# Hybrid encoder trunk, 2 layers on one core: three sets of transposes move from TensorE to Vector

## The chip, the cores and the metric

One core of a Trainium2 chip runs the whole program. The metric is the device time of one execution in microseconds, median of the runs; the kernel before takes 2178.41 us (3 runs, 2178.34 to 2178.55). Lower is better. TensorE, Vector (DVE), Scalar (ACT), GpSimd (POOL) and the DMA queue of SyncE each work through their own instructions in program order and wait for one another by semaphores.

## The reference

`x` is 256 tokens by 2048 channels in float32. Each of the 2 layers has a token mixer and a gated feed-forward part. The mixer's input projection feeds four groups whose outputs are laid side by side and multiplied with `w_out`:

```python
h = rmsnorm(x, norm_mix_pre[l])
proj = h @ w_in[l]
a_q, a_k, a_v, b_glu, c_q, c_k, c_v, d_q, d_k, d_v = jnp.split(proj, split_at, axis=-1)
out_a = diff_attention(a_q, a_k, a_v, diff_lambda[l], diff_subln[l], l)
out_b = conformer_conv(b_glu, ...)      # a * sigmoid(g), 31-tap depthwise conv, layernorm, silu, pointwise
out_c = gqa_axial_attention(c_q, c_k, c_v, gqa_q_norm[l], gqa_k_norm[l])
out_d = neighbourhood_attention(d_q, d_k, d_v, na_rpb[l])
mixed = jnp.concatenate([out_a, out_b, out_c, out_d], axis=-1) @ w_out[l]
x = x + rmsnorm(mixed, norm_mix_post[l])
h = rmsnorm(x, norm_ffn_pre[l])
f = (jax.nn.silu(h @ ffn_gate[l]) * (h @ ffn_up[l])) @ ffn_down[l]
x = x + rmsnorm(f, norm_ffn_post[l])
```

Group A ends in a root-mean-square norm of each head's output; group D is an attention of 4 heads of 128 with a bias. The change touches the input of B's convolution, the output of A, and D's queries and keys.

## The kernel before

**Big products.** Tokens are in two tiles of 128 (`tok` 0 and 1). Every weight slab of 128x1024 is loaded as float32 and split into two single-pass parts: Scalar writes `whi`, Vector writes the rest `wlo` (`split_hi`, `split_lo`). Activations are split in the same way. A step (`products`) is one slab by one token tile: for each of two PSUM banks hi by hi, hi by lo and lo by hi, 6 products of 128x512 into `acc`. Steps come in groups of 3 to 6 slabs, first for token tile 0 and then for tile 1; 7 split slabs are held at once (`NSPLIT`), so Vector may run some slabs ahead of TensorE. The input projection makes the groups in the order B, C, A, D, V (values of A and D); the output projection takes its rows in the order C, B, A, D (`OUT_ORDER`), and a step of it needs the whole output of its group, both token tiles.

**Work beside the products.** The groups' own work is written as generators (`glu`, `conv`, `attn_a`, `attn_d`, `head_d`, `out_a`, `out_d`, ...). After every step `tick` lets each of them issue its next piece up to its next `yield`, if a running estimate of the engines' times (`spend`) says that what it waits for is done. So the order of the instructions of every engine is fixed when the program is written, by these estimates. The 124 taps of the convolution (31 for each of 4 blocks of channels) are Vector instructions that `fill` puts in wherever Vector's estimated time is less than 1.5 us ahead of TensorE's (`CONV_LEAD`). Where a step's input isn't made yet, `wait` ticks the generators until it is, and their instructions then stand on TensorE between two steps with no product in between.

**PSUM.** 4 banks hold `acc`, 2 are for scores (`sc`), 2 for transposes and small products (`tp`); `claim` and `free` count them.

**Transposes.** What has tokens on partitions and is needed with channels on partitions is transposed on TensorE into a `tp` bank (4 blocks of 128x128), and Scalar writes it to SBUF, by Scalar and Vector together where it is split into hi and lo (`split_hi_lo`). One quarter of the tokens' normalised input is turned by Vector instead, in `post` (lines 534 to 540), in 16 instructions of 32 partitions by 128 with 32x32 blocks that go from one quadrant of partitions to another.

**Lines that the change touches.** `glu` (644): Scalar's sigmoid and Vector's product give `u`, lines 657 to 664 transpose it to `uT`, which the taps read. `attn_d` (958): `heads_transposed` makes `qkD` from `rotD`, for queries and keys and two token tiles; then each head makes scores, softmax (`softmax`), transposed probabilities `ptD`. `out_a` (1013): for each token tile the products of probabilities and values go to an `sc` bank, Scalar sums squares (`junk`), GpSimd takes the root `rs`, Vector scales to `oA`, lines 1036 to 1043 transpose and split it to `mixA`. After `conv`'s norm, 4 pointwise groups of 4 products (`tp<-conv,pw`) make `mixB`.

Of the kernel before, what the change touches and what calls it, by code (L numbers as in the profile page):

```python
# [13 lines left out]
AF = mybir.ActivationFunctionType  # L14
# [5 lines left out]
P = 128  # L20
L = 2
S = 256
T = S // P
# [7 lines left out]
PAD = TAPS // 2  # L31
# [71 lines left out]
class Trunk:  # L103
# [461 lines left out]
    def turned(self, l, j):  # L565
# [10 lines left out]
        for tok in range(T):  # L576
            self.mark("h", l, j, tok)


    def layer_consts(self, l):  # L580

        nc, a = self.nc, self.a
        lc = self.slot([2048], F32, "lc")
        v = self.v = {}
        self.l = l
        at = 0

        def part(n, shape):
            nonlocal at
            w = int(np.prod(shape))  # L590
            t = lc[:, at:at + w]
            at += w
            if len(shape) > 1:
                names = "abc"[:len(shape)]
                t = t.rearrange(f"p ({' '.join(names)}) -> p {' '.join(names)}", **dict(zip(names, shape)))
            v[n] = t
            return t

        for n in ("gqa_q_norm", "gqa_k_norm", "diff_subln"):
            part(n, (HD,))  # L600
        nc.sync.dma_start(lc[:, 0:at], a["heads"][l].partition_broadcast(P))
        first = at
        part("dw", (4, TAPS))
        for n in ("conv_dw_b", "conv_ln_g", "conv_ln_b", "conv_pw_b"):
            part(n, (4,))
        nc.sync.dma_start(lc[:, first:at], a["conv"][l])
        yield
        yield
        nc.vector.tensor_scalar(part("subln", (HD,)), v["diff_subln"], 1.0 - self.lam_init(l), None,
                                op0=ALU.mult)  # L610
        for n in ("q", "k"):
            g = v[f"gqa_{n}_norm"]
            cg, sg = part(f"cos_{n}", (T, HD)), part(f"sin_{n}", (T, HD))
            nc.vector.tensor_tensor(cg, self.rope["cos_c"], g.unsqueeze(1).to_broadcast([P, T, HD]),
                                    op=ALU.mult)
            gv = g.rearrange("p (b h w) -> p b h w", b=2, h=2)
            s4 = self.rope["sin_c"].rearrange("p t (b h w) -> p t b h w", b=2, h=2)
            o4 = sg.rearrange("p t (b h w) -> p t b h w", b=2, h=2)
            for h in range(2):
                for t in range(T):  # L620
                    nc.vector.tensor_tensor(o4[:, t, :, h], s4[:, t, :, h], gv[:, :, 1 - h], op=ALU.mult)
# [22 lines left out]
    def glu(self, phase, pair, tok):  # L644
        nc = self.nc
        if tok == 0:
            self.u = self.slot([T, 512], F32, "u")
            self.uT = self.slot([4, S + 2 * PAD], F32, "uT")
            nc.gpsimd.memset(self.uT[:, :, 0:PAD], 0.0)
            nc.gpsimd.memset(self.uT[:, :, PAD + S:], 0.0)  # L650
        av, gv = (self.acc[phase, pair, tok, b] for b in range(2))
        r = self.rstd[:, tok:tok + 1]
        u = self.u[:, tok]
        nc.scalar.activation(u, gv, AF.Sigmoid, scale=r)
        nc.vector.scalar_tensor_tensor(u, av, r, u, op0=ALU.mult, op1=ALU.mult)
        yield
        yield from self.claim("tp")
        b = self.bank("tp", (4, P))
        for c in range(4):
            nc.tensor.transpose(b[:, c], u[:, c * P:(c + 1) * P], self.ident)  # L660
        yield
        nc.scalar.activation(self.uT[:, :, PAD + tok * P:PAD + (tok + 1) * P], b, AF.Copy)
        yield
        self.free("tp")
        self.mark("u", phase)
        if tok == T - 1:
            yield from self.until(T, "u", phase)
            yield
            yield from self.conv()
# [288 lines left out]
    def attn_d(self):  # L958
        qk = self.slot([2, 4, S], F32, "qkD")
        for i in range(2):  # L960
            yield from self.heads_transposed(qk[:, i], lambda t: self.rotD[:, t, i], 4)
        self.ptD = self.slot([4, T, S], F32, "ptD")
        work = self.slot([2, 2, T, S], F32, "workD")
        for h in range(4):
            yield from self.until(h - 1, "done_d", self.l)
            self.spawn(self.head_d(h, qk, work[:, h % 2]))
            yield
# [45 lines left out]
    def out_a(self):  # L1013
        nc, v = self.nc, self.v
        yield from self.until(4, "done_a", self.l)
        self.mixT[0] = self.slot([2, 4, S], F32R, "mixA")
        for t in range(T):
            yield from self.claim("sc")
            b = self.bank("sc", (4, HD))
            for h in range(4):  # L1020
                for c in range(T):
                    nc.tensor.matmul(b[:, h], self.ptA[:, h, c, t * P:(t + 1) * P],
                                     self.vAD[:, c, 0, h * HD:(h + 1) * HD], start=c == 0, stop=c == T - 1)
            yield
            ss, rs = self.small(4, "ss"), self.small(4, "rs")
            for h in range(4):
                self.square_sum(b[:, h], ss[:, h:h + 1], (HD,))
            self.rsqrt(rs, ss, 4, 1.0 / HD)
            o = self.tmp([4, HD], "oA")
            for h in range(4):  # L1030
                nc.vector.scalar_tensor_tensor(o[:, h], b[:, h], rs[:, h:h + 1], v["subln"],
                                               op0=ALU.mult, op1=ALU.mult)
            yield
            self.free("sc")
            yield
            yield from self.claim("tp")
            b = self.bank("tp", (4, P))
            for h in range(4):
                nc.tensor.transpose(b[:, h], o[:, h], self.ident)
            yield  # L1040
            self.split_hi_lo([self.mixT[0][:, i, :, t * P:(t + 1) * P] for i in range(2)], b)
            yield
            self.free("tp")
        self.mark("mix", self.l, 0)


# [134 lines left out]
```

## Time and profile before

| | |
|---|---|
| median of 3 runs | 2178.41 us |
| profiled execution, its own time | 2178.1 us |
| its span, first to last instruction | 2175.9 us |
| TensorE busy | 2154.6 us, 99% of the span |
| Vector busy | 1300.2 us, 60% |
| Scalar busy | 1092.4 us, 50% |
| granted TensorE clock, mean | 0.999 |

The profile is of one execution. Busy times of TensorE come from modelled ends of pipelined products. The helper that records every operation gives all of them line 89, so operations are told apart by what they write and read: `out<-in` by the program's names. A transpose on TensorE is a MATMUL with `ident`; a transpose on Vector is a STREAM_TRANSPOSE. An idle time is put down to the engine whose signal came last. A float32 product of 128x256 is recorded in two parts, so a pointwise group of 4 products has x8.

### The profile page before, as it was taken

Reading aid. Unit: us, or ns where it says so; the run is one execution under the profiler, and the core shown is the slowest. Engines: PE = TensorE matmul, PEld = TensorE weight load, DVE = VectorE, ACT = ScalarE, POOL = GpSimd, SP = SyncE. Lnnn points to the kernel's source line nnn. Section 1 sums busy time; section 2 is a strip of 40 time slices with the busy share of each in tenths; the row PEclk is TensorE's granted clock in tenths of the full one; section 3 lists DMA queues with packets and bytes.
Section 4 is the critical chain, followed back from the end, with each engine's and each line's share of the span. In section 5 each row is a group of like instructions: output and inputs, shape, how many; then the busy total and the mean of one; then the engine's idle time right before and its main releaser. Section 6 shows DMA issues by size and latency. Waiting matters only on the chain.

```text
span 2175.9 us, 25246 instructions
## 1 busy us (share of the span) xinstructions
PE 2154.6 (99%) x9696; PEld 1778.7 (82%) x9696; DVE 1300.2 (60%) x1616; ACT 1092.4 (50%) x1398; POOL 29.9 (1%) x38
## 2 busy tenths in 40 slices
PE   8999999999999999999999999999999999999998
PEld 7888888888888888888878888888888888888886
DVE  5898556755546554444488974566555555454444
ACT  6656755544445444343455577555444444443432
POOL 0000000000000000000000000000000000000000
PEclk9999999999999999999999999999999999999999
DMA  7556446776776666655565563557667666665553
GB/s 277 194 176 185 170 148 223 232 219 210 225 217 220 209 226 216 220 193 193 208 225 187 193 192 136 199 188 251 213 222 223 211 215 222 222 213 213 193 219 130
DMA packets 200281, 447.52 MB, mean 206 GB/s; under 512 B 20704, under 2 KB 43744, under 8 KB 197856
## 3 DMA queue, kind: packets, MB, share of 16 engines
q1 hardware_dynamic: 200016, 445.87, 60.9%
q8 instruction: 76, 1.25, 0.2%
q14 instruction: 45, 0.37, 0.1%
q10 hardware_dynamic: 144, 0.03, 0.0%
HBM read 425.93 MB, written 19.92 MB: 205 GB/s over the span
## 4 chain that ended last, share of the span: by engine, by line
PE 95%; ACT 2%; DVE 1%; issue 1%; DMA 1%; DVEq 0%; POOLq 0%; ACTq 0%; SPq 0%
PE acc L89 91%; PE tp L89 3%; PE sc L89 1%; ACT whi L89 1%; DVE wlo L89 1%; ACT workA L89 0%; DMA lc<-in_heads_dram 0%; ACT L89 0%; DVE mx L89 0%; ACT xT L89 0%; DVE xt L89 0%; DMA x<-in_x_dram 0%; ACT conv L89 0%; ACT junk L89 0%; DVE xT L89 0%
## 5 line engine op out<-in xcount | busy, mean ns | idle before, releaser
L89 PE MATMUL acc<-whi,xT 128*128 128x512 f32 x4096 | 1292.7, 393 | 5.4 <-ACT xT L89 2.4
L89 PEld LDWEIGHTS acc<-whi,xT 128*128 128x128 f32 x4096 | 770.0, 188 | 169.5 <-ACT xT L89 3.5
L89 PE MATMUL acc<-wlo,xT 128*128 128x512 f32 x2048 | 799.4, 390 | 2.6 <-DVE wlo L89 2.6
L89 ACT ACTIVATE whi<-raw,gains 128x1024 fp32r<-128x1024 f32 x512 | 580.5, 1150 | 365.3 <-PE acc L89 334.3
L89 DVE SCALAR_TENSOR_TENSOR wlo<-raw,gains,whi 128x1024 fp32r<-128x1024 f32 x512 | 641.7, 1278 | 188.9 <-ACT whi L89 180.9
L89 PEld LDWEIGHTS acc<-wlo,xT 128*128 128x128 f32 x2048 | 385.3, 188 | 81.9 <-DVE wlo L89 4.4
L89 DVE TENSOR_TENSOR wlo<-raw,whi 128x1024 fp32r<-128x1024 f32 x240 | 292.6, 1223 | 260.5 <-ACT whi L89 243.8
L89 PE MATMUL acc<-whi,hT 128*128 128x512 f32 x1408 | 434.1, 389 | 0.0
L89 ACT ACTIVATE whi<-raw 128x1024 fp32r<-128x1024 f32 x240 | 253.7, 1061 | 304.1 <-PE acc L89 304.0
L89 PEld LDWEIGHTS acc<-whi,hT 128*128 128x128 f32 x1408 | 264.3, 188 | 55.0
L89 PE MATMUL acc<-wlo,hT 128*128 128x512 f32 x704 | 273.9, 389 | 0.0
L89 PEld LDWEIGHTS acc<-wlo,hT 128*128 128x128 f32 x704 | 132.1, 188 | 27.3
L89 DVE TENSOR_TENSOR hT<-ht,hT 128x1024 fp32r<-128x1024 f32 x22 | 27.0, 1226 | 163.5 <-ACT hT L89 163.5
L89 DVE SCALAR_TENSOR_TENSOR h<-acc,rstd,h 128x512 f32<-128x512 f32 x44 | 33.1, 751 | 113.4 <-ACT h L89 113.4
L89 DVE SCALAR_TENSOR_TENSOR conv<-uT,lc,conv 128x256 f32<-128x256 f32 x240 | 99.4, 481 | 0.0
L89 ACT ACTIVATE hT<-ht 128x1024 fp32r<-128x1024 f32 x22 | 23.3, 1059 | 128.7 <-DMA ht<-h_blocks 128.7
L89 ACT ACTIVATE h<-acc,rstd 128x512 f32<-128x512 f32 x44 | 30.3, 689 | 80.5 <-PE acc L89 80.3
L89 ACT ACTIVATE junk<-acc 128x512 bf16<-128x512 f32 x32 | 19.0, 595 | 55.9 <-PE acc L89 53.0
L89 PE MATMUL acc<-whi,mixC 128*128 128x512 f32 x128 | 44.7, 402 | 0.0
L89 DVE TENSOR_TENSOR mg<-acc,gpost 128x512 f32<-128x512 f32 x32 | 21.3, 686 | 35.8 <-PE acc L89 19.5
L89 PE MATMUL acc<-whi,mixB 128*128 128x512 f32 x128 | 42.2, 397 | 0.0
L89 PE MATMUL acc<-whi,mixD 128*128 128x512 f32 x128 | 41.6, 391 | 0.0
(139 smaller groups left out, 987.4 us busy)
## 6 DMA issues: line engine op xcount, KB each, us to landing
raw<-in_ffn_gate_dram SPq DMA_DIRECT2D x176, 512.0 KB, 3.8
raw<-in_ffn_up_dram SPq DMA_DIRECT2D x176, 512.0 KB, 5.1
raw<-in_ffn_down_dram SPq DMA_DIRECT2D x88, 1024.0 KB, 5.0
raw<-in_w_in_dram SPq DMA_DIRECT2D x63, 1024.0 KB, 5.1
raw<-in_w_out_dram SPq DMA_DIRECT2D x32, 1024.0 KB, 5.0
raw<-in_w_in_dram SPq DMA_DIRECT2D x34, 512.0 KB, 4.7
h_blocks<-blocks SPq DMA_DIRECT2D x44, 256.0 KB, 5.5
ht<-h_blocks SPq DMA_DIRECT2D x88, 128.0 KB, 6.0
```

What stands on the lines that cost most here:

```text
L89: return f(*args, **kw)
```

## The change

A new helper `turn` transposes 4 blocks of 128x128 in SBUF with 16 Vector instructions, 4 to a piece. It takes the place of TensorE's transposes, the `tp` bank and Scalar's copy in three places: `u` to `uT`, `rotD` to `qkD` (queries and keys, each token tile), and `oA` to a new temporary `oT`, from which `mixA` is split.

```diff
+    def turn(self, dst, src):
+
+        src = src.rearrange("p (k n) -> p k n", n=P)
+        for q in range(4):
+            qs = slice(32 * q, 32 * q + 32)
+            for r in range(4):
+                rs = slice(32 * r, 32 * r + 32)
+                self.nc.vector.transpose(dst[qs, :, rs], src[rs, :, qs])
+            yield
...
@@ glu
-        yield from self.claim("tp")
-        b = self.bank("tp", (4, P))
-        for c in range(4):
-            nc.tensor.transpose(b[:, c], u[:, c * P:(c + 1) * P], self.ident)
-        yield
-        nc.scalar.activation(self.uT[:, :, PAD + tok * P:PAD + (tok + 1) * P], b, AF.Copy)
-        yield
-        self.free("tp")
+        yield from self.turn(self.uT[:, :, PAD + tok * P:PAD + (tok + 1) * P], u)
@@ attn_d
-            yield from self.heads_transposed(qk[:, i], lambda t: self.rotD[:, t, i], 4)
+            for t in range(T):
+                yield from self.turn(qk[:, i, :, t * P:(t + 1) * P], self.rotD[:, t, i])
@@ out_a
-            yield from self.claim("tp")
-            b = self.bank("tp", (4, P))
-            for h in range(4):
-                nc.tensor.transpose(b[:, h], o[:, h], self.ident)
-            yield
-            self.split_hi_lo([self.mixT[0][:, i, :, t * P:(t + 1) * P] for i in range(2)], b)
-            yield
-            self.free("tp")
+            ot = self.tmp([4, P], "oT")
+            yield from self.turn(ot, o.rearrange("p h w -> p (h w)"))
+            self.split_hi_lo([self.mixT[0][:, i, :, t * P:(t + 1) * P] for i in range(2)], ot)
+            yield
```

The pieces are issued by the same estimates, so all that follows in a layer's mixer stage can be placed anew. Three places follow.

TensorE, layer 0, at the output projection's change from group C's rows to group B's. Before, one of the pointwise groups (`conv,pw`) and the transposes of a D head's probabilities (`ident,workD`) among the products of C:

```order
L89 MATMUL sc_2293<-vAD_2214,ptA_1624 128x128 x8
L89 MATMUL acc_2284<-whi_2134,mixC_1267 128x512
L89 MATMUL acc_2284<-wlo_2153,mixC_1267 128x512
L89 MATMUL acc_2285<-whi_2134,mixC_1267 128x512
L89 MATMUL acc_2285<-wlo_2153,mixC_1267 128x512
L89 MATMUL acc_2284<-whi_2134,mixC_1267 128x512
L89 MATMUL acc_2285<-whi_2134,mixC_1267 128x512
L89 MATMUL tp_2310<-conv_582,pw_1733 128x256 x4
L89 MATMUL tp_2315<-ident,workD_2145 128x128 x4
```

Afterwards, from the last product of C to the first two of B:

```order
L89 MATMUL acc_2347<-whi_2204,mixC_1289 128x512
L89 MATMUL tp_2406<-conv_674,pw_2044 128x256 x4
L89 MATMUL tp_2439<-conv_674,pw_2044 128x256 x4
L89 MATMUL tp_2448<-ident,workD_2337 128x128 x4
L89 MATMUL tp_2458<-conv_674,pw_2044 128x256 x4
L89 MATMUL sc_2463<-vAD_2189,ptA_1621 128x128 x8
L89 MATMUL tp_2472<-ident,workD_2337 128x128 x4
L89 MATMUL sc_2499<-qkD_1824 128x256 x2
L89 MATMUL tp_2502<-conv_674,pw_2044 128x256 x4
L89 MATMUL tp_2508<-ptD_2336,vAD_2189 128x256 x2
L89 MATMUL sc_2524<-qkD_1824 128x256 x2
L89 MATMUL acc_2264<-whi_2221,mixB_2405 128x512
```

All four pointwise groups moved behind the last product of C.

Vector, layer 0, the first heads of D: from the scaled scores of head 0 (`workD`) to the reciprocal of its sums (`sm`). Before:

```order
L89 SCALAR_TENSOR_TENSOR workD_2145<-sc_2164,bias_1430 128x512
L89 SCALAR_TENSOR_TENSOR mixB_2130<-tp_2173,lc_268,mixB_2130 128x256
L89 TENSOR_REDUCE mx_2190<-workD_2145 128x2
L89 TENSOR_SCALAR mx_2190<-mx_2190 128x2
L89 SCALAR_TENSOR_TENSOR workD_2145<-sc_2179,bias_1430 128x512
L89 TENSOR_REDUCE mx_2208<-workD_2145 128x2
L89 TENSOR_SCALAR mx_2208<-mx_2208 128x2
L89 SCALAR_TENSOR_TENSOR mixB_2130<-tp_2203,lc_268,mixB_2130 128x256
L89 RECIPROCAL sm_2191<-sm_2191 128x2
```

Afterwards (the reciprocal `sm_2389` is two rows further on, behind the first `mixB`):

```order
L89 SCALAR_TENSOR_TENSOR workD_2337<-sc_2354,bias_1431 128x512
L89 TENSOR_TENSOR wlo_2373<-raw_2139,whi_2357 128x1024
L89 STREAM_TRANSPOSE oT_2383<-oA_2325 32x4x32 x4
L89 TENSOR_REDUCE mx_2388<-workD_2337 128x2
L89 TENSOR_SCALAR mx_2388<-mx_2388 128x2
L89 SCALAR_TENSOR_TENSOR workD_2337<-sc_2368,bias_1431 128x512
L89 TENSOR_TENSOR wlo_2397<-raw_2225,whi_2371 128x1024
L89 STREAM_TRANSPOSE oT_2383<-oA_2325 32x4x32 x4
L89 TENSOR_REDUCE mx_2415<-workD_2337 128x2
L89 TENSOR_SCALAR mx_2415<-mx_2415 128x2
L89 TENSOR_TENSOR wlo_2423<-raw_2225,whi_2395 128x1024
```

Three splits and 8 turns of A's first token tile stand there now.

Vector, layer 1, group A's second token tile: from `oA` to `mixA`. Before:

```order
L89 SCALAR_TENSOR_TENSOR oA_10403<-sc_10365,rs_10391,lc_8239 128x128 x4
L89 TENSOR_TENSOR mixD_10231<-tp_10425,mixD_10231 128x256
L89 TENSOR_TENSOR wlo_10453<-raw_10221,whi_10378 128x1024
L89 TENSOR_TENSOR mixD_10231<-tp_10443,mixD_10231 128x256
L89 TENSOR_TENSOR mixA_10235<-tp_10446,mixA_10235 128x4x128
```

Afterwards (after these rows come another split, a reciprocal, a maximum, 8 turns in one row, a reciprocal and `mixA_10312`):

```order
L89 SCALAR_TENSOR_TENSOR oA_10532<-sc_10499,rs_10520,lc_8323 128x128 x4
L89 TENSOR_TENSOR mixD_10515<-tp_10516,mixD_10515 128x256
L89 SCALAR_TENSOR_TENSOR workD_10333<-sc_10545,bias_9438 128x512
L89 TENSOR_TENSOR wlo_10560<-raw_10292,whi_10447 128x1024
L89 STREAM_TRANSPOSE oT_10571<-oA_10532 32x4x32 x4
L89 TENSOR_REDUCE mx_10576<-workD_10333 128x2
L89 TENSOR_SCALAR mx_10576<-mx_10576 128x2
L89 SCALAR_TENSOR_TENSOR workD_10333<-sc_10555,bias_9438 128x512
L89 TENSOR_TENSOR wlo_10585<-raw_10292,whi_10558 128x1024
L89 TENSOR_TENSOR mixD_10515<-tp_10568,mixD_10515 128x256
L89 STREAM_TRANSPOSE oT_10571<-oA_10532 32x4x32 x4
L89 TENSOR_TENSOR wlo_10603<-raw_10423,whi_10583 128x1024
```

The softmax rows of D's heads 2 and 3 moved in between, with 16 turns and three more splits.

## Rows read from the trace of the kernel before

**Rows 1.** The page's busy times by engine, whole span.

```profile
PE 2154.6 (99%) x9696; PEld 1778.7 (82%) x9696; DVE 1300.2 (60%) x1616; ACT 1092.4 (50%) x1398; POOL 29.9 (1%) x38
```

**Rows 2.** Waits of TensorE, whole span: us in total, times, longest.

```profile
PE acc L89 <- DVE wlo L89: 2.6, 4, 0.9
PE acc L89 <- ACT xT L89: 2.4, 4, 0.7
```

**Rows 3.** Busy times by stage: two stretches of each layer's mixer stage.

```profile
core 0: us, PE busy (x) PEld busy (x) DVE busy (x) ACT busy (x) POOL busy (x), PEclk, DMA share, GB/s
60.00:200.00 140.00, 140.00 (x645) 115.39 (x645) 129.59 (x234) 79.40 (x130) 3.80 (x2) 1.00 0.58 192
200.00:285.00 85.00, 84.82 (x429) 70.08 (x428) 47.10 (x78) 61.71 (x128) 2.13 (x3) 1.00 0.45 153
1160.00:1280.00 120.00, 120.00 (x555) 99.16 (x554) 114.64 (x203) 70.27 (x117) 3.79 (x2) 1.00 0.59 193
1280.00:1360.00 80.00, 79.95 (x400) 65.51 (x399) 43.04 (x77) 60.56 (x127) 3.10 (x3) 1.00 0.42 145
```

**Rows 4.** Groups by line, whole span: busy us, mean ns, idle before.

```profile
L89 DVE STREAM_TRANSPOSE xt<-x 32x128 f32<-32x128 f32 x96 | 29.0, 303 | 1.5
...
L89 PE MATMUL tp<-ident,rotD 128*128 128x128 f32 x32 | 4.8, 274 | 0.0
...
L89 ACT ACTIVATE qkD<-tp 128x512 f32<-128x512 f32 x8 | 4.8, 598 | 0.0
...
L89 PE MATMUL tp<-ident,oA 128*128 128x128 f32 x16 | 2.4, 272 | 0.0
L89 PE MATMUL tp<-ident,u 128*128 128x128 f32 x16 | 2.4, 272 | 0.0
...
L89 ACT ACTIVATE mixA<-tp 128x512 fp32r<-128x512 f32 x4 | 2.3, 582 | 0.0
```

**Rows 5.** The chain of waits, 1300 to 1400 us: start, us, what.

```profile
1334.60 1.73 PE tp L89 x8
...
1354.50 0.86 PE tp L89 x4
...
1358.99 0.44 PE tp L89 x4
...
1362.63 1.39 PE acc L89 x6
1364.03 1.78 PE sc L89 x16
```

**Rows 6.** Tile mixB, 240 to 345 us: duration ns min/median/max, first and last start.

```profile
L89 PE MATMUL acc<-whi,mixB x64: 387/389/580, 284.9 to 342.3; 128*128 128x512 f32 x64
...
L89 DVE SCALAR_TENSOR_TENSOR mixB<-tp,lc,mixB x4: 476/484/485, 252.0 to 271.6; 128x256 fp32r<-128x256 f32 x4
```

**Rows 7.** Tile mixA, the same stretch and columns.

```profile
L89 PE MATMUL acc<-whi,mixA x64: 387/389/580, 298.1 to 331.4; 128*128 128x512 f32 x64
...
L89 DVE TENSOR_TENSOR mixA<-tp,mixA x2: 692/692/693, 278.6 to 292.9; 128x512 fp32r<-128x512 f32 x2
```

**Rows 8.** Timeline of Vector, 1325 to 1395 us: start, us, instruction.

```profile
1370.40 1.13 DVE L89 SCALAR_TENSOR_TENSOR oA<-sc,rs,lc 128x128 f32<-128x128 f32 x4 [1.13 <-POOL rs L89]
...
1375.98 0.69 DVE L89 TENSOR_TENSOR mixA<-tp,mixA 128x512 fp32r<-128x512 f32 x1
```

**Rows 9.** Groups of Vector by form, whole span: busy us, mean ns, idle before.

```profile
L89 DVE TENSOR_TENSOR wlo<-raw,whi 128x1024 fp32r<-128x1024 f32 x240 | 292.6, 1223 | 260.5 <-ACT whi L89 243.8
...
L89 DVE SCALAR_TENSOR_TENSOR workD<-sc,bias 128x512 f32<-128x512 f32 x8 | 5.5, 682 | 0.6 <-PE sc L89 0.5
...
L89 DVE TENSOR_REDUCE mx<-workD 128x2 f32<-128x512 f32 x8 | 5.4, 677 | 0.0
...
L89 DVE TENSOR_TENSOR mixD<-tp,mixD 128x256 fp32r<-128x256 f32 x8 | 3.4, 425 | 11.9 <-ACT mixD L89 11.9
...
L89 DVE TENSOR_SCALAR mx<-mx 128x2 f32<-128x2 f32 x16 | 2.7, 170 | 0.6
```

## The prediction

> **What bounds the kernel now.** I read the busy shares first, then what TensorE waited for, then the stages, then single stretches. TensorE is busy 99% of the span, and its waits for other engines on the products add up to a few microseconds [rows 1, 2]: the span is TensorE's own work, so what leaves it is won one for one, and any new wait of TensorE is lost one for one. Vector is busy 60% over the span, but the share by stage is what counts [rows 3]. From 60 to 200 us of the first layer it is busy 129.59 of 140 us (92.6%), because the convolution's taps are put into every gap the planner sees; from 200 to 285 us 47.10 of 85 us. The second layer repeats it: 114.64 of 120, then 43.04 of 80 us. So each layer's mixer stage has Vector nearly full first and about half free afterwards, and the half-free part is where the attention heads, the convolution's norm and the groups' outputs hand work from engine to engine.
>
> **What the change removes.** Per layer 4 transposes for each of 2 tokens of the gated input, 4 for each of 2 tokens of group A's output, and 4 for each of 2 tokens of queries and of keys of group D: 8 groups of 4. The trace has them as 16 rows of u, 16 of oA and 32 of rotD [rows 4]. One group of 4 takes 0.44 us of TensorE in the chain [rows 5], so 16 x 0.44 = 7.1 us leave the bound engine. Scalar loses the evictions of u (4) and of D (8), about 0.6 us each [rows 4], 7 us in all; A's output is still split by Scalar and Vector as before. I cost Scalar's relief at nothing: TensorE was fully busy in those stretches.
>
> **What it adds.** Each group of 4 becomes 16 Vector instructions of 32x128. The same instruction on the same shape is in the trace: 96 of them, 303 ns [rows 4]. That is 16 x 0.303 = 4.85 us per group, 8 groups a layer: 38.8 us a layer, 77.6 us in all. None of it is TensorE's, so it costs nothing as long as what Vector delivers is not late. It is a trade of 0.44 us of TensorE and 0.6 us of Scalar against 4.85 us of Vector. The Trainium skill speaks against it: VectorE: DVE Perf Modes, "Rules for kernel authors", says to transpose 128x128 on TensorE where the result may lie in PSUM. By that page's section "The three transpose paths" a TensorE transpose takes 390 ns and 64 of them 25 us, which with the waits below would give about 2169 us; the trace's 0.44 us for four decides, and the sum goes by it.
>
> **Is Vector's work hidden?** First by capacity [rows 3]. Layer 0, 60 to 285 us: 129.6 + 47.1 + 38.8 = 215.5 of 225 us, 96%. It fits only if Vector hardly waits. The most it held in the long first stretch, where the taps (which wait for nobody) fill it, is 92.6%; at that share 215.5 us take 232.7, 7.7 more than there is. Layer 1, 1160 to 1360 us: 114.6 + 43.0 + 38.8 = 196.5 of 200 us; at the 95.5% of its first stretch 205.7, 5.7 more. That is 13.4 us by which TensorE would have to wait.
>
> Then by place, with the order of the instructions. The output projection takes the groups in the order C, B, A, D. Before, in layer 0, B's last part came at 271.6 us and was first used at 284.9, A's at 292.9 + 0.7 and was used at 298.1 [rows 6, 7]: 13 and 4.5 us to spare. Afterwards the conv's taps end later, because the turns of u stand ahead of them and the turns of D among them, and A's and D's chains have turns in them.
>
> Layer 0, B. All four pointwise products now stand behind the last product of C, with no product between them, where before they were spread between products. TensorE meets three hand-overs there. (1) D's head 0: from its scores to its probabilities' transposes. Vector's queue between holds workD twice, three splits, 8 turns, two maxima and small ones: 2x0.68 + 3x1.22 + 8x0.303 + 2x0.68 + 4x0.17 = 9.5 us [rows 4, 9], and Scalar's exponentials and scalings stand between its maxima and its reciprocals; from the scores on I take 13.8 us (an estimate: Vector's 9.5 and Scalar's turns in between; the queue alone would leave 9.5 - 8.5 = 1 us of wait). TensorE's own rows between: 3 steps of 1.39, one pair of scores 0.86, two pointwise groups of 1.73 [rows 5] = 8.5. Wait 5.3 us. (2) The third pointwise group needs a transpose bank that Vector's second mixB frees, behind 8 turns and two reciprocals, 2.7 us; TensorE has one group of 0.44 to do meanwhile: wait about 2 us. (3) The last pair of scores needs the bank that oA frees; before, oA ended 7.5 us after its product began (1364.03 to 1370.40 + 1.13) [rows 5, 8], and TensorE's rows between are 1.78 + 0.44 + 0.86 + 1.73 + 0.86 = 5.7: wait 1.8 us. Sum 9.
>
> Layer 1, A. B just fits there (its pointwise groups stand two to three steps apart), and A's second token is late. From oA to mixA Vector's queue held before one split and two mixD, 1.22 + 2x0.42 = 2.1 us; now it holds three more splits, 16 turns and the softmax rows of D's heads 2 and 3: 4x1.22 + 2x0.42 + 2x0.68 + 2x0.68 + 16x0.303 + 4x0.17 = 14.0 us [rows 4, 9]. From the product on: 7.5 + 14.0 + Scalar's 0.58 = 22.1 us. TensorE's own rows from that product to the first product of A: 1.78, 6 steps of 1.39, five pairs of 0.86 and two groups of 0.44 [rows 5] = 15.4. Wait 6.7, say 7 us. The same sum for before gives 7.5 + 2.1 + 0.44 + 0.58 = 10.6, so mixA at 1374.6; the trace has it at 1375.98 [rows 8].
>
> The two ways agree: 13.4 and 16. I take 16, since the second names the places. The wait of a queue is not confined to them: behind a turn stand splits (wlo) that TensorE needs, and a softmax maximum that Scalar needs; the seven weight buffers cover a split that is a few microseconds late, and I cost that at nothing while the backlog stays under the wait above.
>
> Ends: nothing waits, all 38.8 us a layer lie in Vector's gaps: -7.1 us. Or Vector, in the second stretch, gets done only what it did before, since its gaps are others' chains and cannot be filled: 38.8 - 10.4 free in the first stretch = 28.4 us a layer, 56.8 - 7.1 = +50 us.
>
> **Sum.** -7.1 + 9 + 7 = +8.9 us. The profiled execution took 2178.1 us (span 2175.9 and 2.2 around it), the median of the runs is 2178.41, so the two can be taken as one: 2187.3 us, 2187.
>
> **Rivals.** About 0.2%, 4.4 us, is what a measurement of this kernel can tell from no change: below 2174.0 is faster, above 2182.8 slower.
> (a) All hidden: 2178.4 - 7.1 = 2171.3. For it: Vector has 37.9 us idle in 200:285 and 37 in 1280:1360 [rows 3], a layer's turns 38.8, and part goes before. Against: 4.5 us to spare at A, and the pointwise groups that moved behind the last product of C. It holds while the waits stay under 2.7 us: chance 0.08.
> (b) The waits eat the gain: the hand-overs overlap more than I reckon (one of the two places hidden, or half of each), waits 3 to 11 us, 2174 to 2183, in the middle 2178. For it: three of my hand-overs are 2 us or so each, within the error of such sums. Chance 0.17.
> (c) Forecast, waits 11.5 to 30 us: 2183 to 2201. Chance 0.57.
> (d) Vector becomes the bound of the stage: its backlog grows through the turns of D until the splits come late too, so that TensorE stops at wlo and not only at B and A. It decides from where the backlog is more than the seven buffered splits hide. For it: 96% in the stretch, and every turn is one more instruction ahead of a split. Against: in the stretch at 92.6% TensorE waited for wlo only 2.6 us in the whole span [rows 2]. Price: from 30 us of waits up to the 56.8 above, 2201 to 2228. Chance 0.18.
> Faster 0.08, same 0.17, slower 0.57 + 0.18 = 0.75. The range from 2174 to 2211 leaves out (a) and the upper half of (d), about 0.16.
>
> **What would show it.** Right: TensorE's instructions fall by 64, its busy time by some 7 us or its idle time rises past that; a row of idle time of TensorE before a pointwise product, a workD transpose or the first mixB near 285 to 300 us, and before mixA near 1375; Vector over 90% from 200 to 285 us; 256 new turns of about 303 ns. Waits for mixB or its chain should be near 9 us in layer 0 and for mixA near 7 us in layer 1. Wrong: TensorE still 99% busy with no idle row in these stretches (then a), or its idle rows named wlo, all through 200 to 300 us (then d). If a turn from quadrant to quadrant takes clearly more than 303 ns with these operands, all of Vector's sums rise with it.

## The result, and the profile after

The changed kernel takes **2202.82 us** (median of 4 runs, 2202.64 to 2202.99) against 2178.38 us before: 24.4 us slower, ratio 1.0112 with a 95% interval of 1.0095 to 1.0130. The forecast was 2187, range 2174 to 2211: slower was right, the size was 8.9 us in place of 24.4.

The page of the changed kernel, busy times and the share of each engine in the chain that ended last; the first row answers to [rows 1]:

```profile
PE 2159.8 (98%) x9632; PEld 1776.3 (81%) x9632; DVE 1377.5 (63%) x1872; ACT 1080.4 (49%) x1382; POOL 31.4 (1%) x38
...
PE 77%; DVE 15%; ACT 3%; issue 2%; DMA 2%; POOL 0%; SPq 0%; DVEq 0%; ACTq 0%; POOLq 0%
```

TensorE has 64 instructions fewer, Vector 77.3 us more, as predicted. But TensorE's busy time rose by 5.2 us although its work shrank, and its idle time (span 2200.9 less 2159.8, 41.1 us) rose by 19.8 us from 21.3. These two are the 25.0 us by which the profiled span grew.

The new turns, groups of Vector by form (busy us, mean ns | idle before):

```profile
L89 DVE STREAM_TRANSPOSE qkD<-rotD 32x128 f32<-32x128 f32 x128 | 38.7, 302 | 1.9
...
L89 DVE STREAM_TRANSPOSE uT<-u 32x128 f32<-32x128 f32 x64 | 19.5, 304 | 1.0
L89 DVE STREAM_TRANSPOSE oT<-oA 32x128 f32<-32x128 f32 x64 | 19.3, 302 | 0.9
```

What TensorE waited for in the whole span (total, times, longest), answering to [rows 2]:

```profile
PE tp L89 <- ACT workD L89: 12.8, 4, 3.9
...
PE acc L89 <- DVE wlo L89: 3.0, 4, 0.9
PE sc L89 <- ACT workA L89: 2.2, 4, 1.2
...
PE tp L89 <- ACT ptD L89: 1.6, 1, 1.6
PE tp L89 <- DVE workA L89: 1.4, 2, 1.0
```

The waits for the splits (`wlo`) hardly moved. The new ones are the probabilities of D (`workD`, which Scalar writes last, after Vector's reciprocal) and, smaller, A's softmax. Where they lie, in TensorE's timeline (start, us, instruction, idle before it and who ended that):

```profile
239.31 0.70 PE L89 MATMUL sc<-qkA 64*128 64x256 f32 x2 [1.23 <-ACT workA L89]
...
282.94 1.12 PE L89 MATMUL tp<-ident,workD 128*128 128x128 f32 x4 [3.41 <-ACT workD L89]
285.65 3.41 PE L89 MATMUL tp<-conv,pw 128*128 128x256 f32 x8 [1.59 <-ACT ptD L89]
...
290.69 0.60 PE L89 MATMUL tp<-ident,workD 128*128 128x128 f32 x4
...
295.02 1.13 PE L89 MATMUL sc<-qkD 128*128 128x256 f32 x4 [0.28 <-DVE oA L89]
...
1373.52 1.04 PE L89 MATMUL tp<-ident,workD 128*128 128x128 f32 x4 [2.91 <-ACT workD L89]
...
1396.57 0.84 PE L89 MATMUL tp<-ident,workD 128*128 128x128 f32 x4 [3.86 <-ACT workD L89]
1400.06 1.12 PE L89 MATMUL tp<-ident,workD 128*128 128x128 f32 x4 [2.65 <-ACT workD L89]
```

Two things are to be seen. The waits are at the places of the prediction (the three hand-overs at B in layer 0, and ahead of A's first product in layer 1) and at two that it did not have: A's softmax (239.31) and D's head 0 in layer 1 (1373.52). At 285.65 the profile names Scalar's `ptD`, which ended at 285.60; Vector's second `mixB`, which the prediction named, ended at 285.63, so the trace doesn't tell the two apart. And the instruction behind a wait takes longer: a pointwise group of 8 took 1.73 in the chain before [rows 5] and takes 1.89 at 291.99 here, but 3.41 behind that wait. The windows of 1 us show why (busy of TensorE, its weight loads, Vector, Scalar, GpSimd; then the granted clock):

```profile
284.00:285.00 1.00, 0.06 (x1) 0.00 (x0) 0.96 (x4) 1.00 (x3) 0.00 (x0) 0.50 0.53 209
285.00:286.00 1.00, 0.35 (x1) 0.35 (x2) 0.53 (x2) 1.00 (x3) 0.00 (x0) 0.50 0.00 0
286.00:287.00 1.00, 1.00 (x3) 0.82 (x3) 0.69 (x1) 0.12 (x1) 0.00 (x0) 0.50 0.07 16
287.00:288.00 1.00, 1.00 (x4) 0.72 (x4) 0.00 (x0) 0.00 (x0) 0.00 (x0) 0.50 0.00 0
288.00:289.00 1.00, 1.00 (x5) 0.85 (x4) 0.00 (x0) 0.00 (x0) 0.00 (x0) 0.72 0.00 0
```

The granted clock is at 0.50, the 1.2 GHz level, while TensorE is busy again. In 25 such windows of the two mixer stages it is under 0.97; busy time times the missing share of the clock adds up to 7.7 us. Before, none was under 0.97 in these stages. TensorE's busy time grew by 12.3 us beyond its work (5.2 + 7.1); with the 7.7 taken off, an estimated 4.6 are left. Four transposes behind a wait are recorded longer than four without one at the full clock too (0.84 at 1396.57, granted clock 1.00, against 0.60 at 290.69). That all of the 4.6 us lie in such groups is not shown.

Vector by stage, answering to [rows 3]:

```profile
60.00:200.00 140.00, 139.60 (x634) 114.12 (x633) 132.76 (x248) 75.04 (x119) 3.80 (x2) 1.00 0.57 189
200.00:285.00 85.00, 77.91 (x360) 61.48 (x358) 73.98 (x167) 55.77 (x118) 3.61 (x3) 0.96 0.50 173
...
1280.00:1360.00 80.00, 78.85 (x381) 62.98 (x380) 71.26 (x154) 53.27 (x113) 3.08 (x3) 1.00 0.53 182
```

In 200:285 it is 87% busy, not over 90% as predicted: it waits itself, in its own order, for instance 1.34 us for Scalar's `mixB` at 281.73.

### The profile page after: what moved, and what is told of

Read it like the earlier page. It is cut to its first block, busy times and chain, and to the rows that moved or that the text cites. A ratio compares the mean times of both kernels' runs of the same rounds, so it can differ in the third digit from the quotient of the medians.

```text
span 2200.9 us, 25365 instructions
## 1 busy us (share of the span) xinstructions
PE 2159.8 (98%) x9632; PEld 1776.3 (81%) x9632; DVE 1377.5 (63%) x1872; ACT 1080.4 (49%) x1382; POOL 31.4 (1%) x38
## 3 DMA queue, kind: packets, MB, share of 16 engines
q8 instruction: 75, 1.23, 0.2%
## 4 chain that ended last, share of the span: by engine, by line
PE 77%; DVE 15%; ACT 3%; issue 2%; DMA 2%; POOL 0%; SPq 0%; DVEq 0%; ACTq 0%; POOLq 0%
PE acc L89 76%; DVE wlo L89 6%; DVE conv L89 4%; ACT whi L89 1%; PE tp L89 1%; DVE qkD L89 1%; DVE mx L89 1%; DMA raw<-in_w_in_dram 1%; DVE oT L89 1%; ACT workA L89 1%; DVE rope L89 0%; DVE rotC L89 0%; DVE rotA L89 0%; DMA lc<-in_heads_dram 0%; DVE uT L89 0%
## 5 line engine op out<-in xcount | busy, mean ns | idle before, releaser
L89 PE MATMUL acc<-whi,mixB 128*128 128x512 f32 x128 | 44.2, 410 | 0.0
L89 DVE TENSOR_TENSOR mg<-acc,gpost 128x512 f32<-128x512 f32 x32 | 21.3, 686 | 35.7 <-PE acc L89 19.5
L89 PE MATMUL acc<-whi,mixA 128*128 128x512 f32 x128 | 41.7, 400 | 0.0
```

What stands on the lines that cost most here:

```text
L89: return f(*args, **kw)
```

## The experiments

Ratios are to the kernel before, timed in the same set; idle is TensorE's, span less busy (21.3 us in the kernel before).

| kernel | median us | to before | ratio (95%) | idle us |
|---|---|---|---|---|
| whole change | 2202.82 | +24.4 | 1.0112 (1.0095 to 1.0130) | 41.1 |
| only_u | 2183.84 | +5.6 | 1.0024 (1.0014 to 1.0035) | 25.8 |
| only_d | 2192.10 | +13.8 | 1.0062 (1.0045 to 1.0079) | 32.8 |
| only_a | 2185.86 | +7.6 | 1.0034 (1.0021 to 1.0047) | 28.1 |
| taps11 | 2191.12 | +12.8 | 1.0060 (1.0045 to 1.0075) | 35.3 |
| turn_local | 2181.30 | +2.8 | 1.0013 (1.0003 to 1.0022) | 27.7 |
| warm | 2198.72 | +20.2 | 1.0092 (1.0077 to 1.0107) | 29.1 |
| cost303 | 2226.36 | +47.8 | 1.0218 (1.0201 to 1.0235) | 57.8 |
| only_u303 | 2194.20 | +15.7 | 1.0072 (1.0057 to 1.0087) | 32.8 |
| cost_turn | 2210.50 | +32.2 | 1.0148 (1.0133 to 1.0163) | 47.0 |
| u_cost | 2182.85 | +4.5 | 1.0021 (1.0012 to 1.0031) | 26.8 |
| d_cost | 2188.21 | +9.9 | 1.0045 (1.0030 to 1.0060) | 32.4 |
| d_merge | 2208.39 | +30.1 | 1.0136 (1.0119 to 1.0153) | 44.2 |

**One part at a time.** Each kernel is the one before with the helper `turn` and one of the three edits:

```diff
 only_u:
+        yield from self.turn(self.uT[:, :, PAD + tok * P:PAD + (tok + 1) * P], u)
 only_d:
+                yield from self.turn(qk[:, i, :, t * P:(t + 1) * P], self.rotD[:, t, i])
 only_a:
+            yield from self.turn(ot, o.rearrange("p h w -> p (h w)"))
```

> Only the convolution's gated input is turned by Vector; A's output and D's queries and keys stay on TensorE. TensorE loses 4 groups of 0.44 us, 1.8 us; Vector gains 9.7 us a layer. Theory 'capacity' (the time is lost because Vector has more to do in the mixer stage than the stage is long): layer 0 then holds 176.7 + 9.7 = 186.4 us in 225, 83%, so nothing waits: 2176.6 us. Theory 'hand-overs' (the time is lost where TensorE stands at a group's output that comes late, whatever Vector's share): the planner puts three of the four pointwise groups of layer 0 behind the last product of C, as in the whole change, so TensorE waits there some 3 to 6 us, with the slow clock behind it up to 8, and hardly in layer 1, where the pointwise groups stay two steps apart: 2179 to 2184 us.

> Only D's queries and keys are turned by Vector. TensorE loses 8 groups of 0.44 us, 3.5 us; Vector gains 19.4 us a layer, the largest part. Theory 'capacity': layer 0 holds 196.1 us in 225, 87%, layer 1 177.1 in 200, 88%; nothing waits, 2174.9 us; if any part alone fills Vector it is this one. Theory 'hand-overs': the pointwise groups stay among the products as before, so B is in time in both layers; only the last heads of D move towards D's own rows (transposes of probabilities two or so behind the last product of A), a wait of 0 to 4 us a layer: 2175 to 2183 us.

> Only group A's output is turned by Vector. TensorE loses 4 groups of 0.44 us, 1.8 us; Vector gains 9.7 us a layer. Theory 'capacity': 186.4 of 225 us, 83%, and 167.4 of 200: nothing waits, 2176.6 us. Theory 'hand-overs': 0.44 us of TensorE in A's chain become at least 4.85 us of Vector, against 4.5 us to spare in layer 0 and 4 or so in layer 1, with splits and softmax rows queued between: TensorE stands before the first product of A 2 to 6 us a layer, with the slow clock behind it up to 8: 2180 to 2192 us.

Each part alone is slower, by 5.6, 13.8 and 7.6 us, together 27.0 against 24.4 for the whole. "Capacity" fails in all three, most clearly in only_d, which it put at 2174.9. "Hand-overs" holds for u (2179 to 2184; its waits at B are 1.14, 1.42, 1.01 and 0.69 us) and A (2180 to 2192; a wait ahead of A's first product in each layer, 3.29 and 3.22 us) and fails for D: 13.8 us where it gave at most some 5. only_d's waits of TensorE are not D's alone:

```profile
PE tp L89 <- DVE workA L89: 4.6, 2, 2.9
PE tp L89 <- ACT workD L89: 3.3, 1, 3.3
...
PE tp L89 <- ACT ptA L89: 2.2, 1, 2.2
```

The largest is A's softmax. Vector's timeline in only_d just ahead of it, and TensorE's row that waits:

```profile
235.96 1.28 DVE L89 SCALAR_TENSOR_TENSOR wlo<-raw,gains,whi 128x1024 fp32r<-128x1024 f32 x1
237.26 1.26 DVE L89 STREAM_TRANSPOSE qkD<-rotD 32x128 f32<-32x128 f32 x4
238.56 1.29 DVE L89 TENSOR_REDUCE mx<-sc 128x2 f32<-128x512 f32 x2
239.88 0.17 DVE L89 TENSOR_SCALAR mx<-mx 128x4 f32<-128x4 f32 x1
239.96 1.23 DVE L89 STREAM_TRANSPOSE qkD<-rotD 32x128 f32<-32x128 f32 x4
241.22 0.88 DVE L89 SCALAR_TENSOR_TENSOR workA<-workA,sm 128x256 f32<-128x256 f32 x2
...
241.76 0.98 PE L89 MATMUL tp<-ident,workA 128*128 128x128 f32 x4 [2.94 <-DVE workA L89]
```

D's turns, which nobody waits for yet, stand ahead of `workA`, which TensorE waits for: 8 of them, 2.5 us, in these rows. So the theory had to be made wider: a turn delays every chain that goes through Vector's queue behind it, not only its own group's. In only_a the plain case is seen, 16 turns between `oA` and `mixA`. Vector's first, then TensorE's row:

```profile
299.57 1.13 DVE L89 SCALAR_TENSOR_TENSOR oA<-sc,rs,lc 128x128 f32<-128x128 f32 x4 [1.12 <-POOL rs L89]
...
302.63 3.79 DVE L89 STREAM_TRANSPOSE oT<-oA 32x128 f32<-32x128 f32 x12
...
307.14 0.79 PE L89 MATMUL acc<-whi,mixA 128*128 128x512 f32 x1 [3.29 <-ACT mixA L89]
```

The product behind that wait took 0.79 us, and the next three 0.63 each, where 0.39 is usual: the granted clock is 0.50 there (308 to 310 us).

**Vector's load taken away.** The convolution's loop takes each third tap:

```diff
-        for j in range(TAPS):
+        for j in range(0, TAPS, 3):
```

> The whole change, but the convolution leaves out 20 of its 31 taps in each block (the sums of its remaining taps alone). That takes about as much from Vector in a layer's mixer stage (80 instructions, some 38 us) as the change adds (38.8 us); the chains through B, A and D keep their turns. Theory 'capacity': Vector then has what it had before, so the gain stands: 2171 to 2174 us. Theory 'hand-overs': the place at B is gone (the taps end early, the pointwise groups stand among the products), but A's second token and the last heads of D still come late in both layers, as its chain is as long as before: 2180 to 2192 us.

2191.1 us: the time is within "hand-overs" and far from "capacity". The edit takes 61.2 us from Vector (1377.5 to 1316.3), less than the 76 reckoned, but in the stretches of [rows 3] Vector has about what it had before: 179.2 us in 60:285 against 176.7, and 155.6 in 1160:1360 against 157.7. It is idle 16.1 us in 200:285 and 16.5 in 1280:1360, more than in the whole change. One stop of TensorE, at D's last heads behind A's second token, is longer than any in the whole change, though its idle time in all is shorter (35.3 for 41.1). The order of the instructions is a new one here too, so this run speaks against "capacity" and doesn't by itself measure the turns:

```profile
200.00:285.00 85.00, 84.24 (x398) 68.94 (x397) 68.87 (x146) 51.53 (x99) 1.01 (x1) 1.00 0.51 173
...
1280.00:1360.00 80.00, 79.53 (x379) 63.74 (x377) 63.54 (x127) 49.01 (x97) 1.01 (x1) 1.00 0.53 177
...
302.08 1.33 PE L89 MATMUL tp<-ident,workD 128*128 128x128 f32 x5 [7.81 <-ACT workD L89]
```

**The same order, shorter turns.** Every engine's order is kept, and a piece of a turn is one instruction that stays inside the quadrants:

```diff
-            for r in range(4):
-                self.nc.vector.transpose(dst[qs, :, rs], src[rs, :, qs])
+            self.tc.nc.vector.transpose(dst[:, q, :], src[:, q, :])
+            for r in range(4):
+                self.spend("DVE", "transpose", 128, (), {})
```

> The whole change with the same order of TensorE's instructions and of every other engine's, but each piece of a turn is one Vector instruction of 128x128 that transposes only inside each quadrant (the cross-quadrant moves of the blocks are left out), charged to the planner like the four it stands for. So only Vector's time for a turn falls, from 16 x 0.303 = 4.85 us to perhaps 0.8 to 1.2 us for four blocks, some 30 us a layer. Theory 'turns in Vector's queue' (what TensorE waits for comes late because turns stand ahead of it in Vector's queue): the waits for workD, workA and ptD nearly go, and the gain of 7.1 us on TensorE stays: 2171 to 2178 us. Theory 'order' (the planner put the pointwise products and D's last heads with no product between them, and the chain through Scalar and TensorE itself is too long there, turns or not): most of the waits stay, 2188 to 2200 us.

2181.3 us, between the two and near the first: 21.5 of the 24.4 us are gone. The instructions took 295 to 303 ns each, so four make 1.2 us where the 16 made 4.85:

```profile
L583 DVE STREAM_TRANSPOSE qkD<-rotD 128x128 f32<-128x128 f32 x32 | 9.6, 303 | 0.0
...
PE tp L89 <- ACT workD L89: 5.4, 4, 1.7
...
PE tp L89 <- ACT ptD L89: 1.2, 1, 1.2
```

The five large waits shown above fell from 14.4 us (3.41 + 1.59 + 2.91 + 3.86 + 2.65) to 6.6 (1.15, 1.20, 1.24, 1.71, 1.29 at the same instructions). Since no engine's order differs, the length of the turns in Vector's queue makes most of the loss. What is left, 6.6 us of waits and 1.7 us of half clock, is laid to the order and the chains' other links. The lost gain of 7.1 us and the 2.8 measured make 9.9, so some 1.6 us of it are not placed.

**The clock.** 53 dummy products fill waits, in four places (the expectation says five; the wait at 285.65 got none):

```diff
+        for _ in range(warm):
+            self.tc.nc.tensor.matmul(b[:, 0, 0:P], self.ident, self.ident, start=True, stop=True)
```

> The whole change, and in five of the waits of TensorE (one near 283 us, one near 1373, 1396 and so on) dummy products of 128x128 with the identity into unused or soon overwritten bank space, 53 of them, so that TensorE works through most of the time that it otherwise idles; nothing else is moved. Theory 'clock' (about a quarter of the loss is the half clock that is granted after those waits): the windows behind the waits stay at 1.00 and about 6 us come back, the 3.9 near 241 and the rest not: 2195 to 2198.5 us. Rival 'waits alone' (the slow products behind a wait are no loss of their own, something else ends the stretch): 2202 to 2205 us.

2198.7 us (2197.80 to 2200.15), 4.1 under the whole change, at the upper end of "clock" (2195 to 2198.5) and below the rival. The two were timed in different sets, and their intervals against before overlap, but no run of one lies in the range of the other; the spans of the two profiled executions differ by 2.8 us. The windows behind the waits near 1396 us, first the whole change, then with the dummies:

```profile
1398.00:1400.00 2.00, 0.00 (x0) 0.00 (x0) 1.39 (x5) 0.50 (x2) 0.00 (x0) 0.50 1.01 414
...
1402.00:1404.00 2.00, 2.00 (x6) 1.63 (x5) 0.56 (x2) 0.38 (x1) 0.00 (x0) 0.50 0.00 0
```

```profile
1398.00:1400.00 2.00, 1.76 (x13) 1.14 (x12) 0.38 (x2) 1.55 (x4) 0.00 (x0) 1.00 0.54 219
...
1402.00:1404.00 2.00, 2.00 (x10) 1.67 (x9) 0.00 (x0) 0.00 (x0) 0.00 (x0) 1.00 0.00 0
```

In layer 1 the clock no longer falls (4.1 us of the 7.7 were there); near 285 us the wait without dummies, 1.87 us here, still had the half clock behind it, so layer 0 gave nearly nothing.

**The planner's charge.** The planner takes 0.203 us for an instruction of a turn. Two kernels charge the true 0.303 us for every 32x128 transpose, three more for the new turns alone:

```diff
 cost303, only_u303:
+            if op == "transpose" and n == 128:
+                cost = 0.303
 cost_turn, u_cost, d_cost:
+            if op == "transpose" and n == 128 and self.turning:
+                cost = 0.303
```

> The whole change, but the planner charges a turn's instruction with the 0.303 us that the trace shows in place of 0.203. Theory 'the planner's estimate' (the pieces are placed too early since 256 instructions are each taken for 0.1 us less than they take, 13 us a layer): placed by the true time TensorE's waits mostly go: 2180 to 2191 us. Rival 'the chains are too long' (the turns delay D and A by their real length wherever they are placed; a true estimate moves the wait from one place to another): the pointwise groups spread a little in layer 0, but three of the four transposes of D's probabilities in layer 1 now stand right behind the last product of A: 2195 to 2207 us.

> Only the gated input is turned by Vector, and the planner charges its turns with 0.303 us. In the order the pointwise groups of layer 0 then stand two steps apart instead of three together, with D's heads spread between. Theory 'order at the hand-over': the 4.4 us of waits and 1.6 us of half clock near 283 to 293 us go, and what is left is the gain of 4 groups: 2176 to 2179 us. Rival (the convolution's end, 10 us later, is what TensorE waits for, wherever the groups stand): 2181 to 2185 us, as with the cheaper charge.

Both missed: 2226.4 and 2194.2 us, above all that was expected. The charge also fell on the turns of the normalised input (`xt`), and part of the loss is there: in cost303

```profile
PE tp L89 <- ACT workD L89: 18.9, 4, 7.1
PE acc L89 <- ACT xT L89: 6.3, 6, 3.5
PE tp L89 <- DVE mixC L89: 6.1, 3, 4.1
PE acc L89 <- DVE xT L89: 5.4, 5, 3.4
```

TensorE waits 11.7 us for `xT` in place of 2.4 + 1.3 before. So the charge was put on the new turns alone.

> The whole change, and only the new turns are charged with 0.303 us by the planner (the transposes of the normalised input keep their old charge of 0.203, which the earlier test had raised as well and which made layer 1 start with waits for xT). In layer 0's mixer stage the order is then the one of that test, in which TensorE idled 18 us and ran 5 us worth at the half clock; that part of it stays. Theory 'chains too long' (a true charge moves the waits, it doesn't remove them): 2203 to 2216 us. Rival 'the planner's estimate' (the extra time of the test was the charge on xT alone): 2185 to 2197 us.

> Only the gated input is turned by Vector, with 0.303 us charged for these turns alone. Layer 0 has the order that the test with both charges had (waits of 3.9 us in the mixer stage, no half clock, against 4.4 and 1.6 with the cheaper charge); in layer 1 the pointwise groups now move to the last product of C (two of them with no product between). Theory 'chains too long': the gain in layer 0 and a new wait of 0 to 6 us in layer 1 cancel: 2180 to 2187 us. Rival 'the planner's estimate': 2176 to 2179 us.

> Only D's queries and keys are turned by Vector, with 0.303 us charged for these turns alone. Neither the pointwise groups nor A's second token stand without a product between, in either layer; D's heads lie one to four steps later than with the cheaper charge. Theory 'Vector's queue' (turns stand ahead of what group A's softmax and the splits need, and Vector works in order): the waits for workA stay, the one for workD goes: 2182 to 2190 us. Rival 'the planner's estimate' (with the true charge the pieces are issued when Vector is free for them): 2175 to 2180 us.

2210.5, 2182.9 and 2188.2 us: all three within "chains too long" or "Vector's queue", none near the other. A true charge makes the whole change 7.7 us slower, u alone the same within its interval, D alone 3.9 us faster (in another set), with the wait for A's softmax still there (`workA` 6.3 us in d_cost) and the one for `workD` gone, as "Vector's queue" had it. So the charge, a third too low, is not what makes the whole change slow; of D's 13.8 us it accounts for 3.9. Why the better estimate gives a worse order in the whole change isn't settled.

**Fewer, longer turns.** D's queries and keys of a token tile are turned together:

```diff
+                    self.nc.vector.transpose(both[qs, :, at:at + 32], src[rs, :, qs])
```

> The whole change, but D's queries and keys of one token tile are turned together: 16 instructions of 32x256 per tile in place of 32 of 32x128. If a turn costs what its free size costs (128 columns 303 ns, 512 columns 706 ns on this kernel's other transposes, so by a line between them 437 ns for 256), Vector has 5.4 us a layer less to do, and D's queries and keys need 8 pieces in place of 16, so D's heads start about 8 steps earlier. Theory 'turns in Vector's queue': fewer waits for workD, 2190 to 2200 us. Rival 'order' (all four pointwise groups, and most of D's last heads, stand behind the last product of C in layer 1 too, where they were spread before): 2200 to 2215 us.

```profile
L89 DVE STREAM_TRANSPOSE qkD<-rotD 32x256 f32<-32x256 f32 x64 | 27.9, 436 | 1.0
...
PE sc L89 <- ACT vAD L89: 7.9, 2, 4.9
PE tp L89 <- ACT ptD L89: 6.1, 2, 4.1
```

The instruction costs what was reckoned (436 ns, 437 expected), Vector has 10.8 us less in all, and the kernel is 5.6 us slower than the whole change. The time is where "order" put it, and in layer 1 all four pointwise groups do stand behind the last product of C; but the largest waits, 7.9 us for `vAD`, are at rows that "order" did not name. Less work on Vector in another order was no gain here. No version beat the kernel before. Whether some order of Vector's instructions lets the full turns keep the gain stays open.

## Why the prediction was right in direction and short in size

- **The gain, -7.1 us.** Most of it is seen: 64 instructions fewer, and with short turns TensorE's busy time is 2150.4, 4.2 us less than before with 1.7 us of half clock in it, so 5.9 us.
- **The price, 256 turns of 303 ns.** Measured 302 to 304. By the Trainium skill (VectorE: DVE Perf Modes, "Rules for kernel authors") a 128x128 transpose is TensorE's where PSUM will do; this trace agrees, with 24.4 us.
- **Capacity, 13.4 us.** Wrong as a reason. It agreed with the second way by chance: only_d, which it saw as fitting, lost 13.8 us, and taps11, with 16 us free in the stretch, 12.8.
- **Layer 0, 9 us at B.** The hand-overs are there and shorter: 3.4 for 5.3, 1.6 for 2, 0.3 for 1.8. What I left out is A's softmax behind D's turns (226 to 240 us: 1.03, 1.23 and 0.22). With 0.5 of small ones the stage has 8.3 us. That this is near 9 is luck: the three hand-overs are 5.3 of it.
- **Layer 1, 7 us at A.** 3.86 + 2.65 = 6.5 us, but seen at D's last probabilities, which stand ahead of A's first product on TensorE. "B just fits there" was wrong: D's head 0 cost 2.9 us at 1373.52. With 1.1 at A's softmax the stage has 10.5 us.
- **The splits at nothing.** Right: 3.0 us for 2.6. The time, 2202.8, lies where I put rival (d), but not its mechanism: TensorE doesn't stop at `wlo`.
- **The step that failed** is the sum "-7.1 + 9 + 7" with its premise that a wait is lost "one for one", for its idle time alone. The idle time was 19.8 us for 16; but 12.3 us more went into TensorE's busy time, 7.7 of it in instructions at 1.2 GHz behind waits (the kernel with dummies is 4.1 faster) and an estimated 4.6 whose place is only in part shown, in longer groups behind waits. The forecast and these two, 8.9 + 3.8 + 12.3, make the 25.0 us of the spans.

## What to carry to other kernels

Before moving work from the bound engine to one that is idle on average, list what will stand behind it in that engine's queue: every chain that passes there can be delayed, not just the one that is moved, and free time of the queue elsewhere doesn't help. Price a wait of TensorE as its idle time and what it costs behind it, in products at half clock above all; here TensorE's busy time took 12.3 us on top of 19.8. Where a planner sets the order, the order of each variant has to be read anew: the truer charge and the lighter load (cost_turn, d_merge) both made the whole change longer.

## What the hardware showed that was not expected

A float32 transpose on Vector took the same time here for 128 partitions as for 32: 128x128 in 295 to 303 ns and 32x128 in 302 to 304, while 32x256 took 436. So four blocks turned between quadrants, in 16 instructions, cost four times what they cost left in their quadrants, in 4 (4.85 against 1.2 us). By the Trainium skill (VectorE: DVE Perf Modes, "The three transpose paths") Vector transposes 128x128 in bf16 in 311 ns, in 32x32 blocks only; the float32 rows here, 295 to 303 ns, are near that.

The granted clock fell to 0.50 after quite different waits: after one of 2.94 us (only_d, 242 us), after four short ones, of 1.14, 1.42, 1.01 and 0.69 (only_u, 283 to 290 us), and in the whole change after 1.23 and 0.22 (239 to 241 us). It stayed at 1.00 after 1.15 and 1.20 near 272 to 275 us in turn_local, and after 2.84 near 1334 us in d_cost. So the length of the last wait alone doesn't tell in these runs.
